# Two transformer blocks on one core: layer 1's memory keys and values moved into layer 0's fill, SBUF paddings, and a pool mixer whose residual is scaled ahead

## The chip, the cores and the metric

One core of a Trainium2 chip runs one program. The metric is the device time of one execution in microseconds (us), the median of several runs. Engines are named as in the profile: PE (TensorE's matmuls), PEld (its weight loads), DVE (VectorE), ACT (ScalarE), POOL (GpSimd), SP (SyncE, which issues every DMA of this kernel, in order).

## What is computed

The reference, cut to what the change touches; S = 1024 tokens, D = 1024, 256 memory tokens.

```python
memn = rmsnorm(mem, mem_norm_gain)
for l in range(2):
    h = rmsnorm(x, norm_gain[l])
    mk, mv = split(memn @ w_mem_kv[l])        # 4 heads of 128
    ...                                       # l=0: global and window attention; l=1: neighbourhood attention
    ym = memory_attn(qm, mk, mv)
    y = concat([..., ym]) * silu(gate)
    x = x + y @ w_out[l]
x = rmsnorm(x, final_norm_gain)
h = rms_norm(x, norm_mix_g)
x = x + scale * (pool_windows(h) @ w_pool + b)   # the pool mixer: per group of 256 channels a causal mean minus h
h = rms_norm(x, norm_ffn_g)
a = causal_conv(h @ w_in)                        # 2 x 2816 channels
x = x + (silu(gate) * val) @ w_out
```

All products are done in float32: most of them as three matmuls of `float32r` halves (`whi`, `wlo` for a weight, `hh`, `hl` for an activation; mm3 in the code), the pool mixer's as one plain float32 matmul.

## The kernel before

Activations lie transposed: 128 channels on the partitions, tokens along the free axis, in two chunks of 512. A `dense` job loads a weight strip of 128 output channels in tiles of 128x512 (`wraw`, by DMA), casts it to `whi` on ACT (L238), subtracts on DVE to get `wlo` (L138), and then does 3 matmuls per 128 input channels and chunk (L257, L260, L261). An evacuation follows on DVE and ACT.

**Order of work.** The code runs generators: `seq` chains jobs and loads the next one's weights ahead, `weave` mixes two streams by the share of a planned total that each has used up, and a scheduler with a timeline of its own then lays the instructions out on each engine. In layer 0, `weave` mixes `att` (four global pairs of heads, four window pairs, four memory heads) with `fill` (the projections that feed them, the gates `G[0]` to `G[11]`, reloading of finished `y`, and the first part of the output projection).

**Start.** Ahead of that stands a phase of its own. It normalises the input and the memory, makes the first two projections and the values, and then `mem()` runs `mem_kv(0)` and `mem_kv(1)`: for each layer 4 key jobs (8 x 3 matmuls of 256 columns, `ps<-mhi,whi`) and 2 value jobs (`ps<-whi,mhi`), 192 matmuls, 16 weight tiles (`in_wmk`, `in_wmv`), and results written to DRAM as `mk0h`, `mk1h`, `mv0h`, and so on. The tiles `mhi`, `mlo` (normalised memory) and the weight pool of this phase share space with the attention's tiles, which get it when the phase has ended. `att` begins with 32 matmuls `s<-KA,U` of the first global pair (L810, one row maximum `mcg` on DVE behind each), and then goes on to the scores (L550).

**Pool mixer** (`pool_chunk`, once per chunk of 512 tokens, mixed with the last output projection for chunk 0 and with the first 12 FFN jobs for chunk 1). For each of 8 strips: DVE makes `hx` from the residual `xacc`, ACT scales `xacc` by the gain (L1404), POOL multiplies it by the row factor `bf` (L1405), shifted sums follow, then a plain matmul with `in_wpl` (L313, weights through the shared `wraw` buffers), ACT scales its result and adds the bias into `pt` (L1429), and DVE adds `pt` to `xacc` (L1430). `norm_split` then makes the next norm's halves.

**Placement.** Tiles lie one behind another in SBUF in steps of 32 bytes. In the built program most large tiles begin at a multiple of 64 bytes. These do not, but begin 32 bytes past one: `ah`, `al` (the FFN's hidden activations, the moving operands of its second product), the `yh`, `yl` of layer 1's memory heads in `out1`, the tiles `xr` there, one of the two `hz`, and the small constants `onesr` and `two`.

Of the kernel before, what the change touches and what calls it, by code (L numbers as in the profile page):

```python
# [8 lines left out]
F32 = mybir.dt.float32  # L9
F32R = mybir.dt.float32r  # L10
AF = mybir.ActivationFunctionType
ALU = mybir.AluOpType
# [102 lines left out]
def seq(*jobs, depth=1):  # L115

    for i, j in enumerate(jobs):
        first = True
        for c in j:
            if first:  # L120
                for n in jobs[i + 1:i + 1 + depth]:
                    if isinstance(n, Job):
                        n.load()
            first = False
            yield c
# [15 lines left out]
class Build:  # L141
# [57 lines left out]
    def setup(self):  # L199
        nc = self.nc  # L200
        c = self.const = self.pool("const", 1)
        self.ident = c.tile([128, 128], F32, name="ident")
        self.dma(out=self.ident, in_=self.A["ident"])
        self.vecs = c.tile([128, NVEC], F32, name="vecs")
        self.dma(out=self.vecs, in_=self.A["vecs"])
        self.onesr = c.tile([128, 128], F32R, name="onesr")
        self.ones = raw(self.onesr)
        nc.gpsimd.memset(self.ones, 1.0)
        two = c.tile([128, 256], F32R, name="two")
        nc.gpsimd.memset(raw(two), 0.0)  # L210
        nc.gpsimd.memset(raw(two[:, 64:192]), 2.0)
        self.twor = two[:, 64:192]
        self.sel = [two[:, 128:256], two[:, 0:128]]
        self.bd = c.tile([128, 2], F32, name="bd")
        nc.gpsimd.memset(self.bd, 0.0)
        nc.gpsimd.memset(self.bd[0:64, 0:1], 1.0)
        nc.gpsimd.memset(self.bd[64:128, 1:2], 1.0)
        self.small = self.pool("small", 2)
        self.wp = self.pool("wp", 4)
        self.mm = self.pool("mm", 2, PSUM)  # L220
# [6 lines left out]
    def load_w(self, src, n, engs=None):  # L227
# [14 lines left out]
        return res  # L242

    def load_f32(self, src, n):

        res = []
        for o in range(0, n, 512):
            m = min(512, n - o)
            w = self.wp.tile([128, m], F32, tag="wraw", name="w", bufs=self.wp.bufs - 1)
            self.dma(out=w, in_=src[:, o:o + m])  # L250
            res += [w[:, i:i + 128] for i in range(0, m, 128)]
        return res
# [53 lines left out]

    def dense32(self, src, rhs, nk, evac, chunks=(0, 1), ps_pool=None):

        def body(w):
            for c in chunks:  # L310
                ps = (ps_pool or self.mm).tile([128, 512], F32, tag="mm", name="ps")
                for k in range(nk):
                    self.nc.tensor.matmul(ps, w[k], rhs(k, c), start=k == 0, stop=k == nk - 1, skip_group_check=True)  # L313
                self.run_deferred()
                evac(c, ps)
                yield 0.65 * nk
        return Job(lambda: self.load_f32(src, nk * 128), body)
# [680 lines left out]
    def layer0(self):  # L998
# [21 lines left out]
        with ExitStack() as st:  # L1020
# [27 lines left out]

            with ExitStack() as st2:
                P2 = lambda n, b, **k: st2.enter_context(self.tc.tile_pool(name=n, bufs=b, **k))  # L1050
                mp = P2("memp0", 1)
# [5 lines left out]
                macc = mp.tile([128, 256], F32, name="macc")  # L1057
# [9 lines left out]
                def mem():  # L1067
                    yield from seq(*self.mem_kv(0, hi, lo, rcm, rb), *self.mem_kv(1, hi, lo, rcm, rb), depth=2)
# [4 lines left out]
                self.wp = wp  # L1073
            self.ap = P("ap", 1)
# [13 lines left out]
            def att():  # L1088
# [8 lines left out]
                       qm[2], qm[3], G[8], G[9], G[10], G[11], self.y_load(self.y0, range(7), Y), after(self.done, ("y", 7)),  # L1097
                       *self.out_part(A["wo0"], Y, 0, 8, (0, 1), self.evac_x0(self.rp, A["xT"], x1p), range(OSPLIT)))
            with self.pace(0):
                self.drain(weave((att(), 236.0), (fill, 290.0)))  # L1100
# [215 lines left out]
    def out1(self):  # L1316
# [3 lines left out]
        with ExitStack() as st:  # L1320
            P = lambda n, b, **k: st.enter_context(self.tc.tile_pool(name=n + "n", bufs=b, side="right", **k))
            yp = P("yp", 1)
# [46 lines left out]
    def pool_chunk(self, c, accf, accm, gfm, psb, invc, tail):  # L1369
# [24 lines left out]
        keep = []  # L1394
        for g in GORD:
            ds = []
            for kk in range(2):
# [6 lines left out]
                nc.scalar.activation(x, x, AF.Copy, scale=self.v("gf", k))  # L1404
                nc.gpsimd.tensor_tensor(out=x, in0=x, in1=bf, op=ALU.mult)  # L1405
                if c == 0:
                    nc.gpsimd.tensor_copy(tail[:, k, :], h[:, 512:528])
# [15 lines left out]
            for f in range(2):  # L1423
                ft = 2 * g + f

                def evac(_, ps, ft=ft):
                    x = X[:, ft, cs]
                    t = oj.tile([128, 512], F32, tag="df", name="pt", bufs=2)
                    nc.scalar.activation(t, ps, AF.Identity, scale=self.v("ps", ft), bias=psb[:, ft:ft + 1])  # L1429
                    nc.vector.tensor_tensor(out=x, in0=x, in1=t, op=ALU.add)  # L1430
                    self.norm_split(x, "gz", ft, self.hh[:, ft, cs], self.hl[:, ft, cs], accz, ft == 2 * GORD[0], keep if ft in GK[7:] else None)
                yield from self.dense32(A["wpl"][ft], lambda k, c: ds[k], 2, evac, (c,), ps_pool=self.px)
# [5 lines left out]
    def ffn(self, before):  # L1438
# [6 lines left out]
        with ExitStack() as st:  # L1445
            f = st.enter_context(self.tc.tile_pool(name="ff", bufs=2))
            ht = f.tile([128, 44, 2], F32, name="ht", bufs=1)
# [4 lines left out]
            def conv_evac(j, i, kind):  # L1452
                def evac(c, ps):
                    cs = slice(c * 512, (c + 1) * 512)
                    z = f.tile([128, 514], F32, tag="hz", name="hz", bufs=2)
# [206 lines left out]
```

## Time and profile before

| what | value |
|---|---|
| median of 3 runs (lowest, highest) | 2449.55 us (2443.07, 2453.1) |
| the profiled execution: its time | 2446.46 us |
| its span, first to last instruction | 2444.7 us |
| mean granted PE clock, as a share of full | 0.977 |
| PE busy | 2333.7 us (95%) |
| DVE busy | 1729.5 us (71%) |
| ACT busy | 1088.9 us (45%) |
| POOL busy | 925.1 us (38%) |

Busy shares are means over stages with different limits: layer 0's start lies at 0 to 136 us, its weave up to about 800, layer 1 follows up to about 1450, the pool mixer's two chunks lie at 1600 to 1660 and 1697 to 1790, and the rest is the FFN. Matmuls are pipelined, so a busy PE is not a PE at its peak: what one matmul costs in a full stream is the time from its start to the next one's.

### The profile page before, as it was taken

The numbers are of one execution on the slowest core, as the hardware profiler recorded it, in microseconds if no ns is written. First come the engines' busy times: TensorE is split into PE (matmuls) and PEld (weight loads), VectorE is DVE, ScalarE is ACT, GpSimd is POOL, SyncE is SP. The second block draws the span as 40 slices with busy tenths as digits, with TensorE's granted clock in tenths as the row PEclk, the third lists the DMA queues.
The fourth block names the chain that finished last, engine by engine and source line by source line (L and its number), as shares of the span: only waits on it lengthen the run. The fifth ranks groups of instructions, "written<-read, shape, count | busy, mean of one in ns | idle before, by whom it ended". The sixth has DMA issues, their size and how long they took to land.

```text
span 2444.7 us, 32782 instructions
## 1 busy us (share of the span) xinstructions
PE 2333.7 (95%) x11118; PEld 1910.1 (78%) x11118; DVE 1729.5 (71%) x2856; ACT 1088.9 (45%) x2037; POOL 925.1 (38%) x773
## 2 busy tenths in 40 slices
PE   7989999989999999999999999999899999999999
PEld 6966777767878878888888887866678888888887
DVE  6767886777895557777887889598977464646554
ACT  5425555565663445434443445444444131323231
POOL 3117887891120235646674762475600000000000
PEclk9989999999999999999999999999899999999999
DMA  6752234234456566776766656422222111111112
GB/s 206 215 147 65 77 106 134 78 108 132 128 197 208 197 198 180 193 199 177 216 170 189 182 177 230 153 88 72 63 80 80 44 52 45 51 48 48 49 47 91
DMA packets 234111, 312.74 MB, mean 128 GB/s; under 512 B 101815, under 2 KB 119671, under 8 KB 233944
## 3 DMA queue, kind: packets, MB, share of 16 engines
q1 hardware_dynamic: 233944, 310.65, 42.1%
q8 instruction: 88, 1.44, 0.2%
q14 instruction: 79, 0.65, 0.1%
HBM read 223.45 MB, written 87.03 MB: 127 GB/s over the span
## 4 chain that ended last, share of the span: by engine, by line
PE 73%; DVE 12%; DMA 4%; issue 4%; POOL 3%; ACT 2%; SPq 0%; DVEq 0%; POOLq 0%; ACTq 0%
PE ps L260 20%; PE ps L257 20%; PE ps L261 20%; DVE wlo L138 2%; PE s L550 2%; PE o L610 2%; PE s L551 2%; PE o L609 2%; POOL acc L599 1%; POOL pl L138 1%; DVE pl L138 1%; PE s L1218 1%; PE s L810 1%; DVE mcg L811 1%; PE pt L915 1%
## 5 line engine op out<-in xcount | busy, mean ns | idle before, releaser
L257 PE MATMUL ps<-hh,whi 128*128 128x512 f32 x1888 | 749.1, 399 | 18.4 <-ACT hh L411 8.5
L260 PE MATMUL ps<-hl,whi 128*128 128x512 f32 x1888 | 751.1, 398 | 8.4 <-DVE hl L412 7.6
L261 PE MATMUL ps<-hh,wlo 128*128 128x512 f32 x1888 | 751.9, 399 | 3.6 <-DVE wlo L138 2.5
L238 ACT CAST whi<-wraw 128x512 fp32r<-128x512 f32 (+1 forms) x400 | 244.9, 615 | 467.8 <-PE ps L260 375.4
L257 PEld LDWEIGHTS ps<-hh,whi 128*128 128x128 f32 x1888 | 361.7, 192 | 97.7 <-ACT hh L411 8.5
L260 PEld LDWEIGHTS ps<-hl,whi 128*128 128x128 f32 x1888 | 361.6, 192 | 87.4 <-DVE hl L412 9.3
L261 PEld LDWEIGHTS ps<-hh,wlo 128*128 128x128 f32 x1888 | 361.2, 191 | 81.7 <-DVE wlo L138 3.7
L599 POOL TENSOR_TENSOR acc<-acc,p 128x512 f32<-128x512 f32 (+2 forms) x272 | 323.8, 1198 | 238.4 <-ACT p L465 177.4
L138 DVE TENSOR_TENSOR wlo<-wraw,whi 128x512 fp32r<-128x512 f32 (+1 forms) x388 | 327.2, 847 | 73.0 <-ACT whi L238 63.9
L138 POOL TENSOR_TENSOR pl<-p,ph 128x384 fp32r<-128x384 f32 (+1 forms) x160 | 200.9, 1258 | 10.6 <-ACT ph L467 8.9
L1485 DVE TENSOR_TENSOR xacc<-ps,xacc 128x512 f32<-128x512 f32 x96 | 66.3, 691 | 131.4 <-PE ps L261 130.9
L1457 DVE TENSOR_TENSOR hz<-ps,rbc 128x512 f32<-128x512 f32 x88 | 60.6, 690 | 117.9 <-PE ps L261 114.1
L467 ACT CAST ph<-p 128x512 fp32r<-128x512 f32 (+1 forms) x240 | 131.5, 560 | 23.2 <-PE d L628 6.0
L260 PE MATMUL ps<-al,whi 128*128 128x512 f32 x352 | 139.1, 396 | 0.0
L261 PE MATMUL ps<-ah,wlo 128*128 128x512 f32 x352 | 138.7, 396 | 0.0
L257 PE MATMUL ps<-ah,whi 128*128 128x512 f32 x352 | 138.4, 396 | 0.0
L610 PE MATMUL o<-pl,V 128*64 128x512 f32 (+3 forms) x368 | 121.1, 348 | 13.8 <-POOL pl L138 7.3
L1461 ACT ACTIVATE cv<-hz,vecs 128x512 f32<-128x512 f32 x88 | 71.6, 816 | 130.7 <-DVE hz L1457 128.0
L609 PE MATMUL o<-ph,V 128*128 128x512 f32 (+3 forms) x368 | 118.6, 340 | 4.0 <-ACT ph L917 3.3
L465 ACT ACTIVATE p<-p 128x384 f32<-128x384 f32 (+2 forms) x128 | 66.6, 524 | 110.3 <-DVE p L1245 109.9
L465 ACT ACTIVATE p<-s 128x512 f32<-128x512 f32 x112 | 66.5, 596 | 80.7 <-PE s L551 47.8
L138 DVE TENSOR_TENSOR pl<-p,ph 128x512 fp32r<-128x512 f32 x80 | 85.1, 1064 | 21.7 <-ACT ph L467 19.3
(256 smaller groups left out, 4439.2 us busy)
## 6 DMA issues: line engine op xcount, KB each, us to landing
wraw<-in_w SPq DMA_DIRECT2D x116, 256.0 KB, 3.5
wraw<-in_wfi SPq DMA_DIRECT2D x112, 256.0 KB, 2.6
wraw<-in_wo SPq DMA_DIRECT2D x72, 256.0 KB, 3.1
g<-evf SPq DMA_DIRECT2D x48, 256.0 KB, 3.9
wraw<-in_wfo SPq DMA_DIRECT2D x40, 256.0 KB, 2.6
sg<-g SPq DMA_DIRECT2D x32, 256.0 KB, 2.7
y<-O SPq DMA_DIRECT2D x14, 512.0 KB
hl<-y SPq DMA_DIRECT2D x14, 512.0 KB, 9.2
```

What stands on the lines that cost most here:

```text
L138: out_eng.tensor_tensor(out=out, in0=a, in1=b, op=ALU.subtract)
L238: nc.scalar.copy(hi, raw[:, q:q + e])
L257: i = mm(ps, wh, h, start=first, stop=False, skip_group_check=True)
L260: mm(ps, wh, l, start=False, stop=False, skip_group_check=True)
L261: mm(ps, wl, h, start=False, stop=last, skip_group_check=True)
L465: nc.scalar.activation(p, s, AF.Exp)
L467: nc.scalar.copy(ph, p)
L599: nc.gpsimd.tensor_tensor(out=t, in0=t, in1=p[:, x0 - a:x1 - a], op=ALU.add)
L609: mm(o, V[s][:, j, :], P[0][:, x], start=new, stop=False, skip_group_check=True)
L610: mm(o[0:64], V[s][:, j, 0:64], P[1][:, x], start=False, stop=i == touch[g][-1], skip_group_check=True)
L1461: nc.scalar.activation(t, z[:, 2:514], AF.Identity, scale=self.v("cw2", j), bias=self.v("cb", j))
L1485: nc.vector.tensor_tensor(out=x, in0=ps, in1=x, op=ALU.add)
```

## The change

1. `mem_kv(1)` leaves the start and becomes a part of layer 0's `fill`, behind `G[11]` and ahead of the reloading of `y`; `mhi`, `mlo` and `mrb` therefore stay allocated through layer 0. `fill`'s planned total goes from 290 to 313. The scratch for dynamic DMAs at the bottom of SBUF shrinks from 16 KB to 1 KB per partition (every tile moves down by 15 KB).
2. Paddings: `vecs`, `bd`, `ht`, `hz` get longer, and a tile of 32 bytes is put into the pool of `out1`. In the built program `ah`, `al`, `yh`, `yl`, `xr`, `hz`, `onesr` and `two` then begin at multiples of 64 bytes.
3. Pool mixer: POOL multiplies `xacc` by `bf` first; ACT then scales it by the gain and adds the bias in one step; DVE takes the product straight from PSUM, scales it and adds it to `xacc`. `pt` and its ACT step are gone. `in_wpl` gets 4 buffers of its own, loaded ahead.

```diff
-        self.vecs = c.tile([128, NVEC], F32, name="vecs")
+        self.vecs = c.tile([128, -(-NVEC // 16) * 16], F32, name="vecs")[:, 0:NVEC]
...
-        self.bd = c.tile([128, 2], F32, name="bd")
+        self.bd = c.tile([128, 16], F32, name="bd")[:, 0:2]
...
+            mp = P("memp0", 1)
             with ExitStack() as st2:
-                mp = P2("memp0", 1)
...
-                macc = mp.tile([128, 256], F32, name="macc")
+                macc = mx.tile([128, 256], F32, name="macc", bufs=1)
...
-                    yield from seq(*self.mem_kv(0, hi, lo, rcm, rb), *self.mem_kv(1, hi, lo, rcm, rb), depth=2)
+                    yield from seq(*self.mem_kv(0, hi, lo, rcm, rb), depth=2)
...
+            self.ev2 = self.ev
...
-                       qm[2], qm[3], G[8], G[9], G[10], G[11], self.y_load(self.y0, range(7), Y), after(self.done, ("y", 7)),
+                       qm[2], qm[3], G[8], G[9], G[10], G[11], *self.mem_kv(1, hi, lo, rcm, rb), self.y_load(self.y0, range(7), Y), after(self.done, ("y", 7)),
...
-                self.drain(weave((att(), 236.0), (fill, 290.0)))
+                self.drain(weave((att(), 236.0), (fill, 313.0)))
...
+            P("pad", 1).tile([128, 8], F32, name="pad")
             yp = P("yp", 1)
...
+        def fetch(n):
+            for i in GK[len(wpl):n]:
+                wpl[i] = oj.tile([128, 256], F32, tag="wpl", name="wpl", bufs=4)
+                self.dma(out=wpl[i], in_=A["wpl"][i])
+        fetch(4)
...
-                nc.scalar.activation(x, x, AF.Copy, scale=self.v("gf", k))
                 nc.gpsimd.tensor_tensor(out=x, in0=x, in1=bf, op=ALU.mult)
+                nc.scalar.activation(x, x, AF.Identity, scale=self.v("gf", k), bias=psb[:, k:k + 1])
...
-                    nc.scalar.activation(t, ps, AF.Identity, scale=self.v("ps", ft), bias=psb[:, ft:ft + 1])
-                    nc.vector.tensor_tensor(out=x, in0=x, in1=t, op=ALU.add)
...
+                    nc.tensor.matmul(ps, wpl[ft][:, k * 128:(k + 1) * 128], ds[k], start=k == 0, stop=k == 1, skip_group_check=True)
+                fetch(min(len(wpl) + 1, 8))
...
+                nc.vector.scalar_tensor_tensor(out=x, in0=ps, scalar=self.v("ps", ft), in1=x, op0=ALU.mult, op1=ALU.add)
...
-            ht = f.tile([128, 44, 2], F32, name="ht", bufs=1)
+            ht = f.tile([128, 48, 2], F32, name="ht", bufs=1)
...
-                    z = f.tile([128, 514], F32, tag="hz", name="hz", bufs=2)
+                    z = f.tile([128, 528], F32, tag="hz", name="hz", bufs=2)
...
-    nc = bacc.Bacc("TRN2", target_bir_lowering=False, num_devices=1)
+    nc = bacc.Bacc("TRN2", target_bir_lowering=False, num_devices=1, dynamic_dma_scratch_size=1024)
```

What SP issues at the end of the start, ahead of the first loads for the global attention (`U`, `W` from `qa0`, `KB`, `KA` from `ka`), before:

```order
L158 DMA mk1h<-evh 128x256
L158 DMA U<-qa0h 64x1024 x4
L158 DMA W<-qa0l 64x1024 x2
L158 DMA mk1l<-evl 128x256
L158 DMA mk1h<-evh 128x256
L158 DMA mk1l<-evl 128x256
L158 DMA wraw<-in_wmv 128x512 x4
L158 DMA mk1h<-evh 128x256
L158 DMA mk1l<-evl 128x256
L158 DMA mv1h<-evh 128x256
```

and of the change:

```order
L158 DMA mv0h<-evh 128x256
L158 DMA mv0l<-evl 128x256
L158 DMA qa0h<-evh 128x512
L158 DMA qa0l<-evl 128x512
L158 DMA qa0h<-evh 128x512
L158 DMA qa0l<-evl 128x512
L158 DMA U<-qa0h 64x1024 x4
L158 DMA W<-qa0l 64x1024 x2
L158 DMA wraw<-in_w 128x512 x4
L158 DMA W<-mt 1x8x128
```

Layer 1's memory loads and stores are gone from this place, `KB` and `KA` are now loaded ahead of it, and the fill's next weights (`in_w`) follow right behind. On PE, the last memory matmul of the start is followed by 68 of the fill's 512-column matmuls up to the first `s<-KA,U` (35 before).

PE in the middle of the window attention of layer 0 (`s`: scores, `pt`: transposed probabilities, `o`: product with the values, `ps`: fill), before:

```order
L895 MATMUL s<-KA_1633,U 128x384
L896 MATMUL s<-KB_1632,W 128x384
L257 MATMUL ps<-hh,whi 128x512
L260 MATMUL ps<-hl,whi 128x512
L261 MATMUL ps<-hh,wlo 128x512
...
L257 MATMUL ps<-hh,whi 128x512
L609 MATMUL o<-ph,V_1629 128x256 x2
L260 MATMUL ps<-hl,whi 128x512
```

and of the change, at the same product with the values:

```order
L873 MATMUL s<-KA_1278,U 128x384
L874 MATMUL s<-KB_1277,W 128x384
L247 MATMUL ps<-mhi,whi 128x256
L250 MATMUL ps<-mlo,whi 128x256
L251 MATMUL ps<-mhi,wlo 128x256
...
L251 MATMUL ps<-mhi,wlo 128x256
L587 MATMUL o<-ph,V_1274 128x256 x2
L588 MATMUL o<-pl,V_1274 64x256
```

The memory matmuls of 256 columns stand where gates and output projection of 512 columns stood; those have moved to earlier places of the attention. All 192 lie between the middle of the second-last window pair and the end of the last.

ACT in the pool mixer's chunk 1, between casts of FFN weights (`whi`), before:

```order
L1404 ACTIVATE xacc<-xacc,vecs 128x512
L1429 ACTIVATE pt<-ps,psb,vecs 128x512
L238 CAST whi<-wraw 128x512
L1429 ACTIVATE pt<-ps,psb,vecs 128x512
L238 CAST whi<-wraw 128x512
L1178 ACTIVATE hh<-xacc,vecs 128x512
```

and of the change:

```order
L1392 ACTIVATE xacc<-xacc,psb,vecs 128x512
L1447 ACTIVATE cv<-hz,vecs 128x512
L238 CAST whi<-wraw 128x512
L1447 ACTIVATE cv<-hz,vecs 128x512
L238 CAST whi<-wraw 128x512 x2
L1392 ACTIVATE xacc<-xacc,psb,vecs 128x512
L1157 ACTIVATE hh<-xacc,vecs 128x512
```

The steps `pt` are gone and the step on `xacc` has the bias with it. From layer 1's attention up to its end, the order of all engines is the same in both programs.

## Rows read from the trace of the kernel before

**Rows 1.** Busy us of each engine (x instructions) by stretch, clock, DMA share, GB/s.

```profile
core 0: us, PE busy (x) PEld busy (x) DVE busy (x) ACT busy (x) POOL busy (x), PEclk, DMA share, GB/s
101.14:135.69 34.55, 27.23 (x202) 25.91 (x202) 18.04 (x41) 12.03 (x24) 0.00 (x0) 0.90 0.76 232
135.69:177.00 41.31, 38.19 (x154) 27.97 (x153) 32.13 (x65) 9.81 (x17) 7.49 (x6) 0.90 0.45 119
177.00:560.00 383.00, 356.41 (x1482) 272.03 (x1481) 294.89 (x368) 219.55 (x394) 307.17 (x214) 0.96 0.32 96
560.00:740.00 180.00, 167.04 (x896) 140.01 (x897) 147.35 (x382) 110.05 (x302) 34.00 (x40) 0.97 0.48 157
1600.00:1660.00 60.00, 54.32 (x195) 37.38 (x194) 56.55 (x67) 27.68 (x46) 46.26 (x40) 0.94 0.27 84
1697.00:1790.00 93.00, 75.87 (x274) 52.84 (x273) 87.80 (x113) 44.63 (x73) 52.37 (x38) 0.89 0.22 70
1790.00:2396.00 606.00, 606.00 (x2640) 496.86 (x2641) 350.38 (x606) 183.54 (x274) 1.30 (x1) 1.00 0.17 52
```

**Rows 2.** Instruction groups of 101.14 to 135.69 us: busy, mean ns, idle before and releasers.

```profile
L138 DVE TENSOR_TENSOR wlo<-wraw,whi 128x512 fp32r<-128x512 f32 x15 | 10.0, 688 | 4.1 <-ACT whi L238 4.1
L257 PE MATMUL ps<-whi,mhi 128*128 128x256 f32 x32 | 10.0, 311 | 5.7 <-ACT whi L238 5.5 <-DVE evf L439 0.2
L238 ACT CAST whi<-wraw 128x512 fp32r<-128x512 f32 x14 | 8.5, 617 | 7.1 <-DMA wraw<-in_wmv 5.3 <-PE ps L260 1.0 <-DMA wraw<-in_wmk 0.7
```

**Rows 3.** PE in order of time: start us, us, instruction.

```profile
101.57 0.38 PE L257 MATMUL ps<-mhi,whi 128*128 128x256 f32 x1 [0.43 <-DVE evl L455]
...
143.49 0.85 PE L810 MATMUL s<-KA,U 128*128 128x512 f32 x3
...
176.93 0.79 PE L550 MATMUL s<-U,KA 128*128 128x512 f32 x1
```

**Rows 4.** SP's DMA issues in order of time, 110 to 136 us.

```profile
110.21 0.67 SPq L158 DMA_DIRECT2D qa0h<-evh  x1
...
116.10 2.44 SPq L158 DMA_DIRECT2D U<-qa0h  x4
...
121.70 2.71 SPq L158 DMA_DIRECT2D wraw<-in_wmv  x4
...
135.72 0.45 SPq L158 DMA_DIRECT2D KB<-kah  x1
```

**Rows 5.** Stretches, as rows 1, that hold one kind of moving operand: yh, ah, hh.

```profile
1548.46:1570.87 22.41, 22.41 (x97) 17.98 (x96) 14.33 (x16) 11.53 (x19) 14.54 (x12) 1.00 0.57 189
2286.01:2330.81 44.80, 44.80 (x193) 36.07 (x192) 19.07 (x29) 6.95 (x12) 0.00 (x0) 1.00 0.17 52
2330.81:2396.11 65.30, 65.30 (x289) 54.05 (x288) 40.23 (x72) 22.70 (x34) 0.00 (x0) 1.00 0.15 46
```

**Rows 6.** PE in order of time in layer 0's output projection (12 matmuls apart).

```profile
829.70 0.39 PE L260 MATMUL ps<-yl,whi 128*128 128x512 f32 x1
...
832.42 0.39 PE L260 MATMUL ps<-yl,whi 128*128 128x512 f32 x1
```

**Rows 7.** The matmuls that read ah: ns min/median/max, first and last start.

```profile
L257 PE MATMUL ps<-ah,whi x352: 395/396/397, 1802.7 to 2440.2; 128*128 128x512 f32 x176
```

**Rows 8.** Instruction groups of 1575 to 1795 us, as rows 2.

```profile
L313 PE MATMUL ps<-df,w 128*128 128x512 f32 x64 | 33.8, 643 | 9.9 <-DMA w<-in_wpl 5.2 <-DVE df L1417 4.7
L1430 DVE TENSOR_TENSOR xacc<-xacc,pt 128x512 f32<-128x512 f32 x16 | 16.5, 1030 | 3.2 <-ACT pt L1429 3.2
L1429 ACT ACTIVATE pt<-ps,psb,vecs 128x512 f32<-128x512 f32 x16 | 12.2, 768 | 1.2 <-PE ps L313 1.1
L1404 ACT ACTIVATE xacc<-xacc,vecs 128x512 f32<-128x512 f32 x16 | 11.5, 723 | 26.9 <-DVE hx L1403 26.9
L1461 ACT ACTIVATE cv<-hz,vecs 128x512 f32<-128x512 f32 x14 | 11.2, 812 | 9.7 <-DVE hz L1457 7.1 <-PE ps L313 2.5
L1352 DVE TENSOR_TENSOR xacc<-ps,xr 128x512 f32<-128x512 f32 x8 | 5.5, 682 | 2.0 <-PE ps L261 2.0
```

**Rows 9.** The window attention of layer 0, stretches as rows 1.

```profile
640.00:740.00 100.00, 93.97 (x509) 78.83 (x508) 86.35 (x215) 63.54 (x176) 21.41 (x23) 0.97 0.52 177
680.00:690.00 10.00, 10.00 (x56) 8.49 (x55) 9.22 (x27) 6.29 (x19) 2.23 (x3) 1.00 0.79 270
690.00:700.00 10.00, 6.63 (x32) 5.70 (x31) 9.86 (x16) 9.52 (x22) 5.97 (x5) 0.74 0.96 379
```

**Rows 10.** SP's own waits, 715 to 850 us: us in total, times, longest.

```profile
SPq L158 <- DMA x1p<-xr: 25.2, 10, 4.3
```

More of the change, by code (lines that the diff above doesn't have):

```diff
@@ L241, in load_w @@
                 res += [(hi[:, i:i + 128], lo[:, i:i + 128], hi, lo) for i in range(0, e, 128)]
[L242 to L251, printed above, removed]
         return res
@@ L305, in dense @@
         return Job(lambda: self.load_w(src, nk * 128, engs), body, key, getattr(self, "done", None))
[L307 to L317, printed above, removed]
     def held(self, srcs, rhs, nk, chunks, evacs, pools):
@@ L1394, in pool_chunk @@
         keep = []
+        wpl = {}
+        def fetch(n):
[3 more added lines that the diff above has]
+        fetch(4)
         for g in GORD:
@@ L1422, in pool_chunk @@
                 yield 1.0
[L1423 to L1428, printed above, removed]
-                    nc.scalar.activation(t, ps, AF.Identity, scale=self.v("ps", ft), bias=psb[:, ft:ft + 1])
-                    nc.vector.tensor_tensor(out=x, in0=x, in1=t, op=ALU.add)
-                    self.norm_split(x, "gz", ft, self.hh[:, ft, cs], self.hl[:, ft, cs], accz, ft == 2 * GORD[0], keep if ft in GK[7:] else None)
-                yield from self.dense32(A["wpl"][ft], lambda k, c: ds[k], 2, evac, (c,), ps_pool=self.px)
+            for ft in (2 * g, 2 * g + 1):
+                ps = self.px.tile([128, 512], F32, tag="mm", name="ps")
+                for k in range(2):
+                    nc.tensor.matmul(ps, wpl[ft][:, k * 128:(k + 1) * 128], ds[k], start=k == 0, stop=k == 1, skip_group_check=True)
+                fetch(min(len(wpl) + 1, 8))
+                x = X[:, ft, cs]
+                nc.vector.scalar_tensor_tensor(out=x, in0=ps, scalar=self.v("ps", ft), in1=x, op0=ALU.mult, op1=ALU.add)
+                self.norm_split(x, "gz", ft, self.hh[:, ft, cs], self.hl[:, ft, cs], accz, ft == 2 * GORD[0], keep if ft in GK[7:] else None)
+                yield 1.3
         rz = self.rstd([accz] + keep, 4, f"rz{c}", px)
```

## The prediction, made before the changed kernel ran

> **What bounds the kernel now.** I read the page first, then busy times by stretch, then the instruction groups and the order of time in the stretches that the change touches. Over the whole span PE is the engine that ends last, but not everywhere for the same reason. In the FFN (1790 to 2396 us) PE is busy all of the time at the full clock [rows 1]: there only PE's own pace counts. In the pool mixer's two chunks DVE is the limit: busy 56.6 of 60 us and 87.8 of 93, while PE has idle time and a granted clock of 0.94 and 0.89 [rows 1]. In layer 0's weave no engine is full: PE idles 26.6 of 383 us and 13.0 of 180, at clocks of 0.96 and 0.97, with DVE at 77 and 82% and POOL at 80% in the first of the two [rows 1]; every short stall of an engine that works in order costs a little. At the end of the start PE idles 7.3 of 34.6 us at a clock of 0.90 [rows 1], and most of that is one wait: value matmuls for a cast, which waits for the weights `in_wmv` [rows 2]. SP issued those only at 121.7 us, behind the loads of `U` [rows 4].
>
> **The paddings.** They remove no instruction, so the question is whether 32 bytes of offset cost anything. I compared streams of matmuls of one shape and count how far apart they start. In the FFN's second product, whose moving operands `ah`, `al` lie 32 bytes off, 192 take 44.80 us, 233.3 ns each; in its first, with `hh`, `hl` on multiples of 64, 288 take 65.30 us, 226.7 ns [rows 5]. The two differ in more than the address, but there is a control: `yh`, `yl` lie off in `out1` and take 233.4 ns (22.41 us / 96) [rows 5], and in layer 0, where their like lie on multiples of 64, 226.7 ns (832.42 - 829.70 over 12) [rows 6]. So the offset goes with 6.6 ns per matmul. There are 3 x 352 with `ah` or `al` [rows 7] and, by the loops (8 strips x 4 x 2 chunks x 3), 192 with `yh` or `yl`: 1248 x 6.63 = 8.3 us, of which 7.0 in the FFN, where PE is full. Bounds: 7.0 (where `out1` hides its part) to 8.3; I take 8.3. The paddings of the constants and of `hz` I cost at nothing: DVE and ACT have room in the FFN (350 and 184 of 606 us [rows 1]). The smaller scratch moves every tile by 15 KB, which leaves these offsets alone; all DMAs here come from SP; nothing, too.
>
> [...]
>
> **The pool mixer.** On DVE 16 additions `xacc<-xacc,pt`, 1030 ns each, become 16 that read PSUM and one SBUF tile. The nearest such row is `xacc<-ps,xr` in the same stretch, 682 ns [rows 8]: 0.35 us less each, 2.8 us for each chunk. The waits of DVE for `pt`, 3.2 us in all [rows 8], go with it, since the step between PE and DVE is gone. ACT loses 16 x 0.77 us and its step on `xacc` grows from 723 to about 812 ns (the form with scale and bias [rows 8]), -10.9 us net; ACT is busy about half of the time there [rows 1], so this is worth nothing by itself. PE's waits for `in_wpl`, 5.2 us [rows 8], go, because its loads now stand ahead in buffers of their own; these loads are no more than before. `xacc` x `bf` on POOL no longer waits for ACT; only the addition needs it, much later. What of this reaches the end? Lower bound: the DVE time of chunk 1 alone, 2.8 us, since DVE is full there. Upper bound: also all waits, 2 x 2.8 + 3.2 + 5.2 = 14.0 us. I take 8: chunk 0 gets 4 of its load wait (it is 60 us with 5.7 of idle PE), chunk 1 gets 2.8 and half of the 3.2.
>
> [...]
>
> **The move, at the start.** It takes the stretch from 101.14 to 135.69 out: 34.55 us, in which PE was busy 27.23 at a clock of 0.90. A clock of 0.90 is a fifth of the time at half speed, so about 3.5 us of this are the clock's and 23.8 us are the price of the 192 matmuls in a full stream. What comes forward? The first `s<-KA,U` started at 143.5 us [rows 3]; its last input, `KB` and `KA`, was loaded from 135.7 on [rows 4], when the phase had ended and its space came free. In the changed order 68 matmuls of the fill stand ahead of it: 101.1 + 68 x 0.227 + some 2 us for small ones = 118.5 us. By then `U` should be there: it was issued at 116.1, 5.9 us behind the store of `qa0h` at 110.2 [rows 4], with DMAs 76% busy [rows 1]; without layer 1's loads both should come 2 to 3 us earlier. From there to the first scores (176.9 [rows 3]) took 33.4 us, with DVE busy 32.1 of the 41.3 in its row [rows 1]; 33 fewer matmuls of the fill, and their evacuation, fall in it, so I take 30. The scores then start at 148.5, 28.4 us earlier, with the same 96 matmuls of the fill done. Less the 23.8 us that are now owed: +4.6, I take 5. Bounds: `U` lands as late as before (about 123) and the phase keeps its 33.4 us: 20.5 - 23.8 = -3; the phase takes only 25: +10.
>
> **The move, in the weave.** The fill owes 23.8 us of PE, 16 casts, 16 `wlo` of 0.69 us and 12 evacuations. By the changed order it catches up with the old one, per step of attention, by the third window pair. What a denser fill costs has two bounds. The idle time and the clock there lose some 60 us of 563 (39.6 idle, and about 20 from clocks of 0.96 and 0.97). If every us of work goes on costing its share, 23.8 cost 26.3: -2.5. If the pace is set by POOL and DVE, PE's extra work falls into idle time and costs little: up to +18. Against it stands where the 192 land, in the last window pairs: DVE is busy 86 of 100 us there [rows 9], and the moved work brings at most the 18.0 us that DVE was busy in its old stretch [rows 1], for 24 us of PE; with that DVE would be near 90%, and I allow 8 us more of loss, -10 in all. I take +5, nearer to free than to full price, because POOL and DVE run at 80% through 383 us and the work that came forward fills those. On SP, the waits for `x1p` get more numerous by the changed order, but they were there (25.2 us [rows 10]) without cost to PE.
>
> **Sum.** 8.3 + 8 + 5 + 5 = 26.3 us. The profiled execution took 2446.5, so 2420.2; the median of the three runs lies 3.1 above it, so I expect 2423 against 2449.55.
>
> **Rivals.** (a) The offset is not the cause and 233.3 ns stay. For it: operands differ in more than the address. Against: the two readings of `yh`. It gives 2423 + 8 = 2431. (b) The weave gives nothing and the mixer only its lower bound: DVE, 94% busy in chunk 1, goes on setting the time because its contention with POOL (12 other kinds of addition there) stays. For it: DVE's fullness in both places. With -10 for the weave, -3 at the start, 2.8 for the mixer and 8.3: 2451, no change; with 0 for the weave 2441. (c) Slower: in the last window pairs DVE becomes full, PE stalls behind it and its clock falls. One such stretch is there already: at 690 to 700 us, DVE 9.9 and ACT 9.5 of 10, PE did 32 matmuls at a clock of 0.74, 56 in the 10 us ahead [rows 9], a loss of 4 us. If this held over the 100 us in which the moved work lies, 40 us would be lost, and the weave's +5: 2423 + 45 = 2468. It decides where DVE's demand there reaches some 95% over the 100 us; I count about 90. (d) The mixer gives only 2.8, all else as forecast: 2428.
>
> **How the numbers follow.** Forecast 0.68, (a) 0.08, (b) 0.12, (c) 0.05, (d) 0.07. Half a per cent, 12.2 us, is about what a measurement of this kernel can tell from no change. The forecast, (a) and (d) lie below 2437.3; some of the forecast's own spread does not, and all of (b) does not: faster 0.82, same 0.13, slower 0.05. For the range, all upper bounds together would give 2400 and all lower ones 2452; leaving out a tenth on each side, 2405 to 2441.
>
> **What would show it.** Right: the matmuls with `ah` and `yh` at 226.7 ns; the first `s<-KA,U` near 118 us and the first scores near 148; `xacc` from PSUM near 0.68 us, no wait for `wpl`, and both mixer chunks shorter by about 4 us; layer 0's weave longer than before by less than 24 us, counted from the first scores. Wrong: 233 ns after the paddings; PE idle between 101 and 120 us because `U` or weights are late; a PE clock under 0.9 in the last window pairs; a stretch of the unchanged layer 1 that moves by more than 2 us.

## The result, and the profile after

The changed kernel takes 2420.81 us (median of 4 runs, 2420.07 to 2422.32) against 2447.2 us before (4 runs, 2443.07 to 2453.1): a ratio of 0.989, 95% interval 0.987 to 0.991. Forecast were 2423 (2405 to 2441) and "faster". The profiled execution took 2422.32 us, with a span of 2420.5.

The total came out right; the terms under it did not all. I cut both traces at the same landmarks: the first scores, layer 0's first product with `yh`, layer 1 from its first scores to its last row sum, the mixer from the first row sums of chunk 0 to the last row factors of chunk 1, and the FFN from the first to the last product with `ah`. Busy times by stretch, before:

```profile
core 0: us, PE busy (x) PEld busy (x) DVE busy (x) ACT busy (x) POOL busy (x), PEclk, DMA share, GB/s
0.00:176.93 176.93, 148.68 (x904) 130.42 (x904) 123.39 (x218) 78.70 (x142) 39.68 (x31) 0.93 0.62 188
176.93:828.12 651.19, 611.64 (x2809) 485.87 (x2809) 483.27 (x827) 355.73 (x760) 349.09 (x262) 0.97 0.41 130
910.95:1450.50 539.55, 530.47 (x2844) 456.38 (x2845) 418.69 (x723) 246.21 (x479) 339.99 (x331) 0.99 0.67 183
1581.00:1788.00 207.00, 184.95 (x733) 135.65 (x731) 182.49 (x236) 101.98 (x168) 127.02 (x98) 0.93 0.25 77
1802.70:2440.70 638.00, 638.00 (x2785) 522.53 (x2783) 359.55 (x616) 182.68 (x273) 1.30 (x1) 1.00 0.18 57
```

and of the change:

```profile
0.00:147.31 147.31, 125.01 (x712) 105.79 (x712) 110.51 (x192) 66.92 (x119) 40.29 (x31) 0.92 0.61 185
147.31:821.62 674.31, 633.70 (x3000) 509.16 (x3001) 499.78 (x853) 366.26 (x782) 356.06 (x262) 0.97 0.42 134
904.05:1439.93 535.88, 528.72 (x2844) 455.21 (x2845) 418.13 (x723) 246.46 (x479) 340.05 (x331) 1.00 0.66 184
1571.34:1770.26 198.92, 178.16 (x734) 131.41 (x732) 174.52 (x236) 92.30 (x152) 125.78 (x99) 0.97 0.25 79
1783.03:2416.54 633.51, 633.51 (x2784) 522.46 (x2783) 359.32 (x616) 182.71 (x273) 1.29 (x1) 1.00 0.18 57
```

The start gives 29.6 us and the weave takes 23.1 back: +6.5, forecast +10. The mixer gives 8.1, forecast 8. The FFN gives 4.5, forecast 7.0. And layer 1, whose order on every engine is the same, gives 3.7, forecast nothing. That is 22.8 of the 24.2 us between the two spans; the rest lies between the landmarks, 1.9 us of it just behind the mixer.

The start runs as foreseen; PE in order of time in the change (answering to [rows 3]; foreseen were 118.5 and 148.5):

```profile
118.92 0.39 PE L788 MATMUL s<-KA,U 128*128 128x512 f32 x1
...
147.31 0.80 PE L528 MATMUL s<-U,KA 128*128 128x512 f32 x1 [1.01 <-DVE mcg L789]
```

The paddings do not. Stretches of the change that hold `yh`, `ah` and `hh` alone (96, 192 and 288 matmuls; answering to [rows 5]):

```profile
1538.93:1561.45 22.52, 22.52 (x98) 17.94 (x97) 11.82 (x19) 12.11 (x20) 13.35 (x11) 1.00 0.67 214
2263.51:2307.48 43.97, 43.97 (x194) 36.06 (x192) 19.07 (x29) 6.96 (x12) 0.00 (x0) 1.00 0.18 53
2307.48:2372.81 65.33, 65.33 (x290) 54.05 (x288) 40.23 (x72) 22.71 (x34) 0.00 (x0) 1.00 0.16 46
```

`ah` went from 233.3 to 229.0 ns per matmul (43.97 / 192), not to the 226.8 of `hh`; `yh` stayed, at 234.6 in this stretch (22.52 / 96), which holds two waits; all its starts but the waits average 233.3 in the change and 233.4 before. Yet all four tiles now begin at multiples of 64 bytes. So that is not the condition.

In the built programs another quantity follows the pace: the distance between the start of the moving operand and that of its weights, modulo 512 bytes. `hh` has 0 in both programs (226.7); `yh` 32 before and 448 in the change (233 both times); `ah` 480 before (233.3) and 64 in the change (229.0). It is the distance and not the operand's own place: `hh` before and `yh` in the change both begin 448 past a multiple of 512, the one with weights at 448 (226.7 ns) and the other with weights at 0 (233).

The mixer's rows (instruction groups of 1565 to 1778 us, answering to [rows 8]):

```profile
L1413 PE MATMUL ps<-df,wpl 128*128 128x512 f32 x64 | 32.7, 635 | 10.7 <-issue 5.8 <-DVE df L1404 3.4 <-DVE df L138 0.9
L1392 ACT ACTIVATE xacc<-xacc,psb,vecs 128x512 f32<-128x512 f32 x16 | 13.0, 815 | 32.9 <-POOL xacc L1391 32.9
L1416 DVE SCALAR_TENSOR_TENSOR xacc<-ps,vecs,xacc 128x512 f32<-128x512 f32 x16 | 11.5, 739 | 0.0
```

DVE's addition fell from 1030 to 739 ns, PE no longer waits for `in_wpl` by name, and ACT's step costs 815 ns as estimated. But PE's idle time ahead of the plain product did not shrink (9.9 before, 10.7 now).

### The profile page after: what moved, and what is told of

Same layout as the page of the kernel before. It is cut to its first block, busy times and chain, and to the rows that moved or that the text cites. A ratio compares the mean times of both kernels' runs of the same rounds, so it can differ in the third digit from the quotient of the medians.

```text
span 2420.5 us, 32735 instructions
## 1 busy us (share of the span) xinstructions
PE 2318.6 (96%) x11118; PEld 1903.2 (79%) x11118; DVE 1720.2 (71%) x2856; ACT 1078.2 (45%) x2021; POOL 931.0 (38%) x773
## 4 chain that ended last, share of the span: by engine, by line
PE 75%; DVE 11%; DMA 5%; issue 3%; POOL 3%; ACT 2%; SPq 0%; DVEq 0%; POOLq 0%; ACTq 0%
PE ps L247 21%; PE ps L250 21%; PE ps L251 21%; PE o L588 2%; PE s L528 2%; PE o L587 2%; DVE wlo L138 2%; PE s L529 2%; POOL acc L577 2%; DMA sg<-g 1%; DVE mcg L789 1%; PE s L1197 1%; POOL pl L138 1%; DVE R L609 1%; PE s L788 1%
```

## Experiments

Theory D: the pace depends on the distance between moving operand and weights. Theory M (the prediction's): on whether the operand begins at a multiple of 64. Theory P: on the product itself. On the other terms the question was how much of them is the edit and how much one execution's chance. All profiles, cut at the landmarks above (us):

| profile | first scores at | weave | layer 1 | mixer | FFN |
|---|---|---|---|---|---|
| before | 176.9 | 651.2 | 539.6 | 207.0 | 638.0 |
| e1_pads_only | 179.2 | 658.0 | 538.6 | 204.9 | 633.5 |
| e9_scratch | 182.0 | 656.7 | 538.8 | 210.3 | 638.0 |
| e4_move_back | 175.1 | 658.2 | 539.6 | 198.9 | 633.5 |
| e5_no_mem1 | 151.8 | 653.8 | 537.4 | 199.5 | 633.5 |
| the change | 147.3 | 674.3 | 535.9 | 198.9 | 633.5 |
| after_again | 147.3 | 669.1 | 535.4 | 199.1 | 633.5 |
| e6_aligned | 147.5 | 671.7 | 536.2 | 199.0 | 630.8 |
| e2_dose | 147.1 | 674.8 | 537.2 | 199.7 | 636.3 |
| e3_old_mixer | 148.6 | 675.8 | 536.4 | 208.2 | 633.5 |
| e7_residual_only | 148.0 | 672.4 | 543.9 | 203.5 | 633.5 |
| e8_prefetch_only | 148.1 | 666.5 | 537.1 | 203.9 | 633.5 |
| e10_total290 | 148.4 | 679.9 | 541.2 | 198.7 | 630.8 |
| e11_total336 | 148.3 | 686.0 | 536.4 | 198.8 | 630.8 |

**after_again**, no edit. 

> The changed kernel once more, for a second profile and to stand beside the next three on one chip. What it tests: layer 1, whose code the change leaves alone, was 4.1 us shorter in the first profile of the change, 2.4 of them a stretch at half clock near 1059 us of the trace of before. If that is chance of one execution, a second profile may have such a stretch there or elsewhere, and layer 1 differs by 2 us or more between the two. If it belongs to the changed kernel, layer 1 takes 536 us (from its first scores to its last product with the row sums) again, within 0.5. Time near 2421 us.

Measured: 2418.16 us (5 runs, 2417.18 to 2422.24; before on the same chip 2446.58), ratio 0.9889 (0.9874 to 0.9904); layer 1 took 535.4, within 0.5 of the first profile. By the expectation the gain would belong to the change, but two profiles do not settle it: the column above runs from 535.4 to 543.9 with the same code of layer 1 (see e7). The half clock of the first profile of before that the expectation speaks of lies at 1047 us (a clock of 0.66 from 1045 to 1050, 0.50 from 1047.36 to 1049.49), not near 1059.

**e1_pads_only**: the kernel before with the lines of the diff on `vecs`, `bd`, `ht`, `hz` and `pad`. 

> The kernel before with the paddings of the change alone (vecs, bd, ht, hz, and the 32 bytes in the pool of out1). Prediction's term: 1248 matmuls from 233.3 to 226.7 ns, 8.3 us less than before. By what the first profile of the change shows: ah, al at 229.0 and yh, yl still at 233.3, so 1056 x 4.3 ns = 4.6 us less. If the paddings are not what moved the pace: 233.3 everywhere and no change. Beyond that the stretches ahead of the FFN stay as in the kernel before.

Measured: 2439.89 us (12 runs, 2435.98 to 2450.46), ratio 0.9974 (0.9961 to 0.9988), that is 3 to 10 us less; FFN 633.5, `ah` 229.0 and `yh` 233.3 ns. The timed interval holds both figures; the FFN column holds 4.5 alone.

**e6_aligned**: two more paddings.

```diff
-            P("pad", 1).tile([128, 8], F32, name="pad")
+            P("pad", 1).tile([128, 120], F32, name="pad")
...
             al = {}
+            f.tile([128, 112], F32, name="shift", bufs=1)
```

> The changed kernel with two more paddings, so that ah, al, yh, yl start at the same place modulo 512 bytes as the weights they are multiplied with (distance 0; in the change ah, al are at distance 64 and take 229.0 ns, yh, yl at 448 and take 233.3). Theory D, the distance between moving operand and weights sets the pace: all four at 226.7 ns as hh has, so 1056 x 2.3 + 192 x 6.6 ns = 3.7 us less than the changed kernel, near 2417. Theory M of the prediction, a multiple of 64 in the moving operand's own address: all are multiples of 64 before and after this edit, so no change. Theory P, the product itself (its place in PSUM, its evacuation) is slower: no change, 229 and 233 stay.

Measured: 2416.23 us (4 runs, 2415.81 to 2419.46), ratio 0.9881 (0.9865 to 0.9898). The stretches of `yh`, `ah`, `hh` as above:

```profile
1535.15:1557.10 21.95, 21.95 (x97) 17.94 (x96) 11.92 (x19) 12.29 (x20) 13.97 (x11) 1.00 0.69 215
2258.71:2302.23 43.52, 43.52 (x193) 36.04 (x192) 19.06 (x29) 6.96 (x12) 0.00 (x0) 1.00 0.18 54
2302.23:2367.51 65.28, 65.28 (x290) 54.05 (x288) 40.26 (x72) 22.77 (x34) 0.00 (x0) 1.00 0.15 46
```

`ah` takes 226.7 ns (43.52 / 192), exactly as `hh` (65.28 / 288). `yh` takes 228.6 in its stretch, because two starts there waited (265 and 335 ns). Runs of 12 `yh` matmuls show the pace, first in the change (233.3 ns), then in e6 (226.7):

```profile
1566.93:1569.73 2.80, 2.80 (x14) 2.24 (x12) 2.05 (x2) 1.84 (x4) 2.80 (x2) 1.00 0.08 7
1562.54:1565.26 2.72, 2.72 (x13) 2.25 (x12) 1.97 (x2) 1.63 (x4) 2.72 (x3) 1.00 0.08 17
```

D holds, M and P fall. The FFN's second product was never dearer in itself.

**e2_dose**: twelve distances in one kernel.

```diff
-                            al[i] = tuple(f.tile([128, S], F32R, ...
+                            al[i] = tuple(f.tile([128, 1280], F32R, ...
+            DOSE = [(0, 16), (32, 48), (64, 96), (128, 160), (192, 256), (320, 448)]
+            def part(t, i, c):
+                o = c * 640 + DOSE[GROUP[i]][c] // 4
+                return t[:, o:o + 512]
```

> The changed kernel with ah, al placed at twelve distances (0, 16, 32, 48, 64, 96, 128, 160, 192, 256, 320 and 448 bytes, modulo 512) from the weights, one for each chunk of each group of FFN strips; read from the starts of the matmuls, not from the time. Theory D: 226.7 ns at 0, about 233 at 32, 229 at 64, 233 at 448 as seen so far, and the steps between. Theory M: one pace for all the multiples of 64 (0, 64, 128, 192, 256, 320, 448), another for 16, 32, 48, 96, 160. Theory P: the same pace everywhere.

It ran once, 2425.14 us; it is read from starts. A run has 12 matmuls at one distance (8 such runs for most, 5 and 6 for 320 and 448); the median of the runs' means, in ns:

| 32 | 48 | 64 | 96 | 128 | 160 | 192 | 256 | 320 | 448 |
|---|---|---|---|---|---|---|---|---|---|
| 233.3 | 232.8 | 229.9 | 233.5 | 232.5 | 234.5 | 233.4 | 228.5 | 229.0 | 232.5 |

One run each of 64, 96, 192 and 256, as stretches up to the next run's start:

```profile
2013.46:2016.22 2.76, 2.76 (x14) 2.25 (x13) 1.29 (x2) 0.62 (x1) 0.00 (x0) 1.00 0.12 8
2016.22:2019.02 2.80, 2.80 (x14) 2.26 (x13) 0.69 (x1) 0.00 (x0) 0.00 (x0) 1.00 0.23 86
2276.78:2279.58 2.80, 2.80 (x13) 2.24 (x12) 1.29 (x2) 0.62 (x1) 0.00 (x0) 1.00 0.14 11
2279.58:2282.32 2.74, 2.74 (x13) 2.25 (x12) 0.69 (x1) 0.00 (x0) 0.00 (x0) 1.00 0.23 87
```

The run of 256 stands behind one of 192 and falls into two parts, its first five matmuls and its last six:

```profile
2279.58:2280.74 1.16, 1.16 (x7) 0.94 (x6) 0.69 (x1) 0.00 (x0) 0.00 (x0) 1.00 0.55 207
2280.96:2282.32 1.36, 1.36 (x7) 1.13 (x6) 0.00 (x0) 0.00 (x0) 0.00 (x0) 1.00 0.00 0
```

The five take 232 ns on average, the six 226.7 (1.36 / 6), as at distance 0. In the kernel before, `hh` at distance 0 behind `ah` starts in the same way: 230, 236, 228, 232 and 231 ns, then 226.7. So 256 equals 0 (226.7 ns once the first five are past) and 320 equals 64 (229.0 and 229.9): at these distances the pattern repeats after 256 bytes, with 0 best, 64 between, and 32, 48, 96 to 192 dearest (232.5 to 234.5); and behind a change of distance some matmuls cost more (232 ns in the first five, not 226.7). 0 and 16 stood in the first group, where they alternate in runs of six: the first run at 0 takes 226.7 ns, the next ones, each behind a run at 16, take 231.7.

**e9_scratch**: `dynamic_dma_scratch_size=1024` alone on the kernel before. 

> The kernel before with the scratch for dynamic DMAs at 1 KB, nothing else: every tile lies 15 KB lower, the distances between moving operands and weights are the same as before. The prediction costs it at nothing: the time of the kernel before within 0.3%, ah and yh at 233.3 ns. If the place in SBUF as such sets the pace or the traffic of DMA, time or pace move.

Measured: 2448.45 us (10 runs, 2444.82 to 2461.35; before 2448.31), ratio 1.0011 (0.9992 to 1.0031); FFN 638.0, `ah` at 233.3 ns. Costing it at nothing was right as far as this interval shows.

**e3_old_mixer**: `pool_chunk` of the kernel before in the change. 

> The changed kernel with the pool mixer of the kernel before (weights through the shared buffers, the residual scaled first by the gain on ACT, pt and its ACT step, the addition from SBUF). Forecast of the mixer term: 8 us slower than the changed kernel, 4 in each chunk; by the first profiles 7.8, of which 2.7 in chunk 0 and 5.1 in chunk 1, as read between the row sums' first matmuls of the chunks and the last of the second. Rival d: 2.8 us alone. Near 2428.

Measured: 2434.51 us (5 runs, 2429.71 to 2438.61), ratio 0.9936 (0.9915 to 0.9957), 11 us behind the change by the ratios, give or take some 5; mixer 208.2. Four profiles with the old mixer have 204.9 to 210.3 (mean 207.6), six with the new 198.9 to 199.7 (mean 199.2; the two with another planned total left aside): 8.4 us. Rival (d) falls.

**e7_residual_only** and **e8_prefetch_only**: one half of the mixer's edit each.

```diff
 e7
-                nc.tensor.matmul(ps, wpl[ft][:, k * 128:(k + 1) * 128], ds[k], ...)
+                yield from self.dense32(A["wpl"][ft], lambda k, c: ds[k], 2, evac, (c,), ps_pool=self.px)
 e8
-                nc.vector.scalar_tensor_tensor(out=x, in0=ps, scalar=self.v("ps", ft), in1=x, op0=ALU.mult, op1=ALU.add)
+                nc.scalar.activation(t, ps, AF.Identity, scale=self.v("ps", ft), bias=psb[:, ft:ft + 1])
+                nc.vector.tensor_tensor(out=x, in0=x, in1=t, op=ALU.add)
```

> The changed kernel with the mixer's weights through the shared buffers again, while the residual stays scaled ahead and the addition reads PSUM. It splits the mixer's term. By the prediction's working DVE's shorter addition gives 5.6 us and the two waits (in_wpl on PE 5.2, pt on DVE 3.2) the rest: theory DVE, the wait for weights is hidden behind DVE's time and this kernel is as fast as the change (within 1 us), near 2420; theory L, the load's wait is on the path in both chunks, and this kernel is 3 to 5 us slower than the change, near 2424.

> The changed kernel with the mixer's weights in their own buffers, loaded ahead, but with the residual chain of the kernel before (gain on ACT first, pt, the addition from SBUF). Both chunks of the mixer together, from the row sums' first matmuls of chunk 0 to the last row factors of chunk 1, took 199.2 us on average in six profiles with the new mixer, 206.7 in three with the old, 203.5 with the residual alone. If the two parts add up, this kernel takes 202.4 there, near 2423 in all. If DVE's time is what counts and the wait for weights only fills in behind it, this kernel takes 206, near 2427; if the weights' wait is the larger part, 200.

Measured: 2428.03 us (4 runs), ratio 0.9908 (0.9883 to 0.9934), and 2426.37 us (4 runs), ratio 0.9912 (0.9895 to 0.993). The mixer takes 203.5 and 203.9: 4.1 us for the residual and 3.7 for the loading ahead; together 7.8 of the 8.4. This speaks against one being hidden behind the other, but it rests on one profile each, and the four with the old mixer scatter by 5 us. The product's group over the mixer, with the residual alone and with the loading ahead alone:

```profile
L1365 PE MATMUL ps<-df,w 128*128 128x512 f32 x64 | 35.9, 675 | 11.2 <-DVE df L1419 6.0 <-DMA w<-in_wpl 4.5 <-DVE xacc L1430 0.6
```

```profile
L1413 PE MATMUL ps<-df,wpl 128*128 128x512 f32 x64 | 32.7, 636 | 10.7 <-issue 6.2 <-DVE df L138 3.5 <-DVE df L1404 0.8
```

The wait for `in_wpl` is gone in the second, but PE's idle time there is as long, most of it "issue". So the loading ahead seems to pay, but not as less idle time of PE before this product; by what path is left open.

e7 also shows a part of what moves layer 1. In it and in after_again PE meets the same two stalls, the first of them longer in e7; in order of time, e7 first:

```profile
1037.37 0.91 PE L1197 MATMUL s<-KB,U 112*128 112x256 f32 x3 [1.97 <-DMA KB<-kc2h]
1038.08 0.63 PE L247 MATMUL ps<-hh,whi 128*128 128x512 f32 x1
1038.50 0.63 PE L250 MATMUL ps<-hl,whi 128*128 128x512 f32 x1
...
1125.05 0.50 PE L247 MATMUL ps<-hh,whi 128*128 128x512 f32 x1 [2.35 <-DVE evl L1273]
```

```profile
1033.01 0.72 PE L1197 MATMUL s<-KB,U 112*128 112x256 f32 x3 [0.79 <-DMA KB<-kc2h]
1033.57 0.40 PE L247 MATMUL ps<-hh,whi 128*128 128x512 f32 x1
1033.80 0.40 PE L250 MATMUL ps<-hl,whi 128*128 128x512 f32 x1
...
1119.05 0.50 PE L247 MATMUL ps<-hh,whi 128*128 128x512 f32 x1 [2.34 <-DVE evl L1273]
```

The 5 us behind the second stall, e7 and then after_again (stretches as above; the granted clock stands third from the end):

```profile
1125.00:1130.00 5.00, 4.96 (x15) 3.91 (x16) 1.72 (x4) 1.25 (x2) 0.00 (x0) 0.66 1.00 341
```

```profile
1119.00:1124.00 5.00, 4.95 (x23) 4.00 (x23) 2.05 (x4) 1.26 (x2) 0.00 (x0) 1.00 0.98 325
```

The same wait of 2.3 us is followed by matmuls at half clock in one execution (0.66 over these 5 us) and by none in the other (1.00). At half clock, as behind the first stall in e7, starts lie 420 ns apart, in after_again 230. All 14 profiles have this second stall, 2.34 to 2.37 us long; a spell at half clock follows it in nine. By the starts of matmuls in layer 1 (over 400 ns apart at 512 columns), such spells of 5 to 8 matmuls number 3 in e7 (543.9 us), 2 in the kernel before, in e4 and e10 (539.6, 539.6, 541.2), 0 in after_again, e6 and e11 (535.4, 536.2, 536.4), and 1 in the others. The spells do not account for all of it: with one spell each, e1 and e9, which lack the move, take 538.6 and 538.8, and the four with the move 535.9 to 537.2. What else differs is open.

**e4_move_back**:

```diff
-                    yield from seq(*self.mem_kv(0, hi, lo, rcm, rb), depth=2)
+                    yield from seq(*self.mem_kv(0, hi, lo, rcm, rb), *self.mem_kv(1, hi, lo, rcm, rb), depth=2)
...
-                self.drain(weave((att(), 236.0), (fill, 313.0)))
+                self.drain(weave((att(), 236.0), (fill, 290.0)))
```

(and `mem_kv(1)` out of `fill`). 

> The changed kernel with the move undone: mem_kv(1) back at the end of the start, the fill's planned total 290 again; placement, paddings and mixer stay those of the change. Theory S (start): the stretch of the start is entered again, so the first scores come about 30 us later, and the weave, from the first scores to layer 0's first product with yh, takes 16 to 23 us less (651 and 658 us in the kernel before and with paddings only, 669 to 675 in four profiles of the move); net 7 to 13 us slower than the changed kernel, near 2430. Theory W (the weave pays the full price): it gets back 23.8 us or more there, net at most 6 slower, near 2424. On layer 1, whose own code is the same in all: if its gain of about 3 us (535.4 to 537.2 with the change, 538.6 and 539.6 without) came from the move, it is lost here (539); if it came from the placement, it stays (536).

Measured: 2434.25 us (4 runs, 2430.69 to 2435.95), ratio 0.9936 (0.9913 to 0.9958): 11 us behind the change by the ratios, give or take some 5. First scores at 175.1 (28 later), weave 658.2 (16 shorter than the change's first profile). Theory S holds.

**e5_no_mem1**: as e4, but without `mem_kv(1)` in the start, and with `self.mk[1], self.mv[1] = self.mk[0], self.mv[0]`. 

> The changed kernel with layer 1's memory keys and values left out: no mem_kv(1) anywhere, layer 1 reads those of layer 0, the fill's planned total 290. It gives the whole price of the moved work in its new place. In a full PE stream the 192 matmuls cost 23.8 us. Theory F (they fill idle time): the weave from the first scores to layer 0's first yh product gets only 10 to 19 us shorter than the 672 us that four profiles of the change have on average, near 2404 in all. Theory W: 24 us or more, near 2395. Rival c of the prediction (DVE full, clock falls): more than 40.

Measured: 2399.45 us (4 runs, 2396.05 to 2406.85). The weave is 653.8, against 672.1 as the mean of the seven profiles that have the moved work and 313: the moved work costs 18.3 us in its new place, for 23.8 of PE by the prediction's working (192 starts at the usual 120 ns make 23.0). Theory F. The stretch that holds its 192 matmuls, in the change:

```profile
639.44:699.30 59.86, 52.39 (x366) 48.77 (x365) 52.32 (x141) 42.26 (x117) 16.61 (x16) 0.91 0.55 181
```

DVE is busy 87% of it and the clock is 0.91: rival (c)'s point is not reached.

**e10_total290** and **e11_total336**: e6 with `(fill, 290.0)` and `(fill, 336.0)`. 

> The changed kernel with ah, al, yh, yl at distance 0 from the weights and with the fill's planned total left at 290 although it now has layer 1's memory work: the weave then feeds the attention a denser fill, which ends earlier. In six profiles with 313 the stretch from the first scores to layer 0's first product with yh takes 673 us. If a denser fill fills more idle time, this gives a few us less, below 2416; if the attention is what is held up (POOL and DVE at 80% in the global pairs), it gives as much more, near 2420.

> The changed kernel with ah, al, yh, yl at distance 0 and with the fill's planned total at 336 instead of 313 (290 took 679.9 us from the first scores to layer 0's first product with yh, 313 some 673). If the total of 290 was bad because a denser fill holds up the attention and leaves little fill for the memory heads, a thinner fill may gain a few us more, 2413 or below; if 313 is near its best point, this one is slower again, by up to what 290 cost, 2420 to 2428.

Measured: 2430.37 us (4 runs), ratio 0.9931 (0.9913 to 0.9949), and 2426.44 us (6 runs, 2421.94 to 2430.57), ratio 0.9914 (0.9901 to 0.9928). Both lose 8 and 14 us in the weave (679.9 and 686.0): with 290 the global pairs end 12 us earlier but the stretch from the first memory scores to `yh` grows from 129 to 147 us; with 336 that shrinks to 116, but the pairs ahead of it take 27 us more. 313 is the best of the three, and e6 has the lowest median here, though its interval overlaps that of the change.

## Why the prediction was right, and where it was not

- **Paddings, 8.3 forecast, 4.5 measured.** The failed step is "the offset goes with 6.6 ns per matmul", read as a matter of multiples of 64. Both operands of my control (`yh` in layer 0 and in `out1`) differed in the distance to their weights as well, and the control could not tell the two apart. The full cure that I priced exists: at distance 0 the FFN takes 630.8, 7.2 us less than before (forecast 7.0), and `yh` too runs at 226.7. The change takes 4.5 of it and nothing of `yh`, whose 233 ns were a sign of error that I had named. e6 moves all four operands by multiples of 64 and the pace changes all the same (`ah` from 229.0 to 226.7 ns, `yh` from 233.3 to 226.7). No run here tests whether the weight loads are what costs the 2 to 8 ns on top of 227 at other distances; that the reads of operand and weights collide is a reading, not shown.
- **Mixer, 8 forecast, 8.4 measured** (mean of four old against six new). Its working was less good: I gave each chunk about 4, and it is 2.0 in chunk 0 and 6.4 in chunk 1 (means of the same profiles: 97.1 to 95.1 and 110.5 to 104.0, parted at chunk 1's first row sums). And "0.35 us less each" rests on a mean that mixes two things. Duration by instruction (least, median, most), before:

```profile
L1430 DVE TENSOR_TENSOR xacc<-xacc,pt x16: 675/684/1776, 1612.3 to 1774.9; 128x512 f32<-128x512 f32 x16
```

and in the change:

```profile
L1416 DVE SCALAR_TENSOR_TENSOR xacc<-ps,vecs,xacc x16: 735/740/744, 1601.7 to 1761.6; 128x512 f32<-128x512 f32 x16
```

  The usual addition from SBUF took 684 ns, less than the 740 of the new form (forecast 682); a few took up to 1776. The new form is never long. So the source in PSUM went with 56 ns more here, in another form of addition, and the row of 1030 was right on the sum all the same: 4.7 us less in all, 5.6 forecast.

  The trace shows when an addition is long. In the kernel before, all seven above 690 ns began while a tensor operation of POOL was under way, and each ended 546 to 552 ns after that one; the other nine took 675 to 686. In the four other profiles with the old chain every longer one ends so too; five of the short ones run beside a POOL operation that then takes 2.5 to 2.6 us itself, in place of 1.1 to 1.8. One of the seven, and the same place in the change, where two additions pass beside the running POOL operation:

```profile
1633.29 1.74 POOL L1190 TENSOR_TENSOR rbc<-rbc,sq 128x512 f32<-128x512 f32 x1
1633.81 1.78 DVE L1430 TENSOR_TENSOR xacc<-xacc,pt 128x512 f32<-128x512 f32 x1
```

```profile
1609.09 1.74 POOL L1169 TENSOR_TENSOR rbc<-rbc,sq 128x512 f32<-128x512 f32 x1
1609.60 1.40 DVE L1416 SCALAR_TENSOR_TENSOR xacc<-ps,vecs,xacc 128x512 f32<-128x512 f32 x2
```

  By their ends, 546 to 552 ns behind the POOL operation's, the long additions of two SBUF tiles read as if they had waited for it. What would make them wait no run shows.

  But the addition does not explain where the time went. The eight additions of chunk 0 fell from 10.0 to 5.9 us in sum, those of chunk 1 only from 6.5 to 5.9, so the even 2.8 us for each chunk was wrong, and chunk 1 gained most all the same. Chunk 1 before and in the change:

```profile
1678.50:1787.99 109.49, 93.76 (x366) 68.35 (x365) 100.88 (x136) 54.92 (x89) 58.92 (x42) 0.92 0.21 66
1666.17:1770.25 104.08, 90.18 (x368) 65.81 (x367) 99.13 (x135) 49.63 (x81) 57.80 (x42) 0.97 0.20 65
```

  DVE is busy 1.8 us less and the chunk is 5.4 us shorter; PE's granted clock is higher (0.97 against 0.92). By what path chunk 1 gains the rest stays open.
- **Start, +5 forecast.** 5.8 in the first pair (29.6 less 23.8); 30.6 less 23.8 = 6.8 between the means of seven profiles with the move (147.7) and four without (178.3). The lower bound's late `U` did not arise: PE had no wait between 101 us and the first `s<-KA,U`. The half speed in the working of the 23.8 is in the trace of before: the clock is 0.50 from 124.72 to 131.55 us and 1.00 in the rest of 101.14 to 135.69. PE was busy for 3.73 of these 6.83 us, so the clock's part was nearer 1.9 us than 3.5; the 23.0 that 192 usual starts make are near the 23.8 all the same.
- **Weave, +5 forecast.** Only +0.7 in the first pair; but the profile of before has the shortest weave of the four without the move (651.2; 656.7 to 658.2 in the others). Means 672.1 and 656.0: the move costs 16.1 and the term is +7.7. What I had not priced is the planned total: with 290 (e10) the weave takes 8 us more.
- **Layer 1, nothing forecast, 3.7 in the first pair.** My own sign of error ("moves by more than 2 us"). The difference goes in part with half-clock spells behind stalls that come at the same places in all versions; their number differs from execution to execution. Means: 537.4 with the move (seven), 539.2 without (four), inside the scatter of 535 to 544. That the change does something to it is neither shown nor excluded. Behind the same stall (2.35 and 2.34 us) 5 us have 15 matmuls at a clock of 0.66 in e7, and 23 at 1.00 in after_again.
- **Rivals.** (a) was half true, in a form that I had not thought of: the multiple of 64 is not the cause, the distance to the weights is. (b), (c) and (d) fell.

So the mechanism held for the start and, as a sum, for the mixer; for the paddings it did not. That the total came out so near is luck: the paddings gave 4 less, and the move some 4 more by the means; in the first pair of profiles, where the move gave 3.5 less, layer 1's 3.7 stood in for it.

## To carry to other kernels

Place a matmul's moving operand and its weights at the same residue modulo 256 bytes and look at the starts of a long stream: 7 ns on each of 1056 matmuls made 7.2 us here, more than the paddings that only went for multiples of 64 (4.5). Look at what stands ahead in the stream too, since behind a change of distance the next matmuls cost more (five at 232 ns here, where 226.7 is the pace). Before a mean duration goes into a sum, look at its least, median and most: if it hides two populations, look at what else ran when the long ones began. And where a stretch that nothing touched moves, take more profiles before crediting the change.

## What was not expected of the hardware

A 512-column float32r matmul costs 226.7 ns from start to start when operand and weights begin at distance 0 modulo 256 bytes, 229.0 at 64, and 232 to 235 at 32, 48, 96, 128, 160 and 192. Behind a stream at another distance, the first five at distance 0 or 256 still cost 232 on average. In the kernel before, DVE's seven additions of two SBUF tiles that took over 690 ns began beside a running POOL operation, ended 546 to 552 ns after it and took up to 1776 ns; with one source in PSUM, in the change, they took 735 to 744. And behind the same stall of 2.3 us of PE came half clock in some executions (a clock of 0.66 over 5 us in e7) and none in others (1.00 in after_again).
